# Nine pairs of the down projection get high and low part of the weights by DMA, and ten pairs use seven products

## The chip, the cores and the metric

The kernel runs on one core of a Trainium2 chip. The metric is device time in microseconds (us), from one launch of the whole program. Several engines run side by side on the core: TensorE (PE, its weight loads are shown as PEld), VectorE (DVE), ScalarE (ACT), GpSimd (POOL) and SyncE (SP). Each takes its own instructions in the order in which the program lists them. SP, ACT and POOL can also issue DMA transfers; these run on 16 DMA engines that all issuers share.

## The reference

One decoder layer on 256 tokens of width 2048: differential attention beside a pooling mixer, cross-attention into 256 memory tokens, then a SwiGLU feed-forward part with 5632 inner features, and a last RMSNorm. What matters here is the feed-forward part:

```
def _swiglu(h, w_gate, w_up, w_down):
    return (jax.nn.silu(h @ w_gate) * (h @ w_up)) @ w_down
...
hf = _rmsnorm(x, norm_ffn[l])
x = x + _swiglu(hf, w_gate[l], w_up[l], w_down[l])
return _rmsnorm(x, norm_final)
```

The change concerns the product with `w_down` (5632 by 2048), the last large product of the layer.

## The kernel before

All matrix products run in a rounded 32-bit format (float32r). To keep accuracy each operand is split into a high part (the value rounded to that format) and a low part (the value minus the high part), and a product is made of three matmuls: high by high, high by low, low by high. `split` does that: ACT writes the high part (line 129), DVE subtracts it from the source (line 130). `mm3` issues the three matmuls (lines 217 to 219), each 128 by 128 against 512 columns in the down projection.

Down projection: the 2048 output columns are done in two blocks `b` of 1024, and the 5632 inner features are 44 tiles of 128, taken as 22 pairs `p`. For each pair and block one transfer of 1 MB brings four weight pieces of 512 columns each (`raw`, line 706, issued on SP; `raw` has three buffers). `prep` yields split pieces, and the loop at line 783 issues the products:

- An ordinary pair needs 8 block products (2 token halves, 2 column halves, 2 feature tiles), so 24 matmuls. Its weights are two splits of two pieces each (line 719 and 720).
- A pair in `FAST` uses a Strassen-like scheme with 7 block products, so 21 matmuls. Its weights need three sums and differences more on DVE (`less`, line 716), and four splits. The activations of such a pair were combined beforehand in `pair_of`.

In the kernel before, `FAST` is 2, 4, ... 18 (nine pairs); the 13 others are ordinary. So seven-product pairs and ordinary pairs alternate for most of a block. Split weights lie in `whi` and `wlo` with three buffers each. A tile framework adds the waits: an instruction that writes a buffer waits until the readers of its earlier contents are done. The order on each engine is fixed when the program is built.

Of the kernel before, what the change touches and what calls it, by code (L numbers as in the profile page):

```python
# [24 lines left out]
F32 = mybir.dt.float32  # L25
F32R = mybir.dt.float32r
AF = mybir.ActivationFunctionType
ALU = mybir.AluOpType
# [3 lines left out]
P = 128  # L32
# [11 lines left out]
FP = FT // 2  # L44
NB = D // 512

FAST = tuple(range(2, 20, 2))


C_MIX, C_XAT, C_MEM, C_FFN, C_FIN, C_SUB, C_PSC, C_LAM = 0, 16, 32, 48, 64, 80, 82, 90  # L50
# [5 lines left out]
def layer_kernel(ctx: ExitStack, tc: tile.TileContext, a: dict, out: bass.AP):  # L56
    nc = tc.nc
# [23 lines left out]
    def name(n):  # L81
        uid[0] += 1
        return f"{n}{uid[0]}"
# [14 lines left out]
    def t1():  # L98
        return tmp.tile([P, S], F32, tag="t1", bufs=6, name=name("t1_"))
# [235 lines left out]
    v = [values(ps_v0, rc_x), values(ps_v1, rc_x)]  # L335
# [6 lines left out]
    for g, w in enumerate(WINDOWS):  # L342
# [5 lines left out]
        for kt in range(2):  # L348
            b, dgn = t1(), t1()
# [346 lines left out]
    dec = ctx.enter_context(tc.tile_pool(name="dec", bufs=3, side="right", reuse_waits="tile"))  # L696
# [5 lines left out]

    def prep(b, p):

        raw = wts.tile([P, 4, 512], F32, tag="raw", name=name("raw"))
        nc.sync.dma_start(out=raw.rearrange("p s n -> p (s n)"), in_=a["w_dn"][b, p])
        b11, b22, b21, b12 = (raw[:, i] for i in range(4))

        def parts(src, n=2):
            hi = wts.tile([P, 1024], F32R, tag="whi", name=name("whi")).rearrange("p (s n) -> p s n", s=2)  # L710
            lo = wts.tile([P, 1024], F32R, tag="wlo", name=name("wlo")).rearrange("p (s n) -> p s n", s=2)
            split(hi[:, :n], lo[:, :n], src)
            return [(hi[:, i], lo[:, i]) for i in range(n)]

        def less(o, x, y):
            nc.vector.tensor_tensor(out=o, in0=x, in1=y, op=ALU.subtract)

        if p not in FAST:
            yield parts(raw[:, 0:2])
            yield parts(raw[:, 2:4])  # L720
            return
        yield parts(raw[:, 0:2])
        s = dec.tile([P, 2, 512], F32, tag="sum", bufs=2, name=name("sum"))
        less(s, b12[:, None].to_broadcast([P, 2, 512]), raw[:, 0:2])
        yield parts(s)
        less(b12, b22, s[:, 0])
        yield parts(raw[:, 2:4])
        less(b22, b21, b12)
        yield parts(raw[:, 1:2], 1)

    def finished(b, t, h):

# [41 lines left out]
    for b in range(2):  # L774
        M = {}
        C = [acc() for _ in range(4)]

        def into(ps, w, n, p, last=False):
            mm3(ps, sides[p][n], w, id(ps) not in M, last or (p in FAST[-1:] and any(ps is q for q in shared)))
            M[id(ps)] = True  # L780

        shared = [misc() for _ in range(4)] if FAST else []
        for p in range(FP):
            parts = prep(b, p)
            if p in FAST:
                b11, b22 = next(parts)
                into(shared[0], b11, A11, p)
                into(C[1], b22, S4, p)
                s1, s3 = next(parts)
                tick()  # L790
                into(shared[1], s1, S1, p)
                into(shared[3], s3, S3, p)
                b21, s2 = next(parts)
                into(C[0], b21, A12, p)
                into(shared[2], s2, S2, p)
                s4, = next(parts)
                tick()
                into(C[2], s4, A22, p)
            else:
                b11, b22 = next(parts)  # L800
                tick()
                into(C[0], b11, A11, p)
                into(C[2], b11, A21, p)
                into(C[1], b22, A12, p)
                into(C[3], b22, A22, p)
                b21, b12 = next(parts)
                tick()
                last = p == FP - 1
                into(C[0], b21, A12, p, last)
                into(C[1], b12, A11, p, last)  # L810
                into(C[2], b21, A22, p, last)
                into(C[3], b12, A21, p, last)
            if p == 8 or (not FAST and p == 0):
                between.append(load_rows(b))
            if b == 1 and p == 9:
                between.append(load_gains())
            if p in FAST[-1:]:
                between.append(sums(b, [shared[0], None, shared[1], shared[2], shared[3]]))
        finish()
        for i, ps in enumerate(C):  # L820
            y = ys[b][i // 2][:, (i % 2) * 512:(i % 2 + 1) * 512]
            nc.vector.tensor_tensor(out=y, in0=ps, in1=y, op=ALU.add)
            if b:
                finished(b, i // 2, i % 2)
        if b == 0:
            def late():
                for _ in range(26):
                    yield

                nc.scalar.activation(out=ss[:, :, 0], in_=ss[:, :, 0], func=AF.Sqrt)  # L830
                for i in range(4):
                    finished(0, i // 2, i % 2)
                    yield
            nc.vector.memset(ss, 1.0)
            between.append(late())
# [90 lines left out]
```

## Time and profile before

| | |
|---|---|
| median of 3 runs | 1423.15 us (1422.8 to 1424.44) |
| the profiled execution's own time | 1424.28 us |
| its span, first to last instruction | 1422.6 us |
| PE busy | 1404.4 us, 99% |
| DVE busy | 967.5 us, 68% |
| ACT busy | 742.3 us, 52% |
| POOL busy | 23.6 us, 2% |
| mean DMA rate | 193 GB/s |

Busy time of PE overlaps from one matmul to the next, so it is not a sum of costs: what a matmul costs when many follow each other is the distance between their starts. The granted TensorE clock was 1.00 of full speed (2.4 GHz) through the stage that is changed.

### The profile page before, as it was taken

Reading aid. Unit: us, or ns where it says so; the run is one execution under the profiler, and the core shown is the slowest. Engines: PE = TensorE matmul, PEld = TensorE weight load, DVE = VectorE, ACT = ScalarE, POOL = GpSimd, SP = SyncE. Lnnn points to the kernel's source line nnn. Section 1 sums busy time; section 2 is a strip of 40 time slices with the busy share of each in tenths; the row PEclk is TensorE's granted clock in tenths of the full one; section 3 lists DMA queues with packets and bytes.
Section 4 is the critical chain, followed back from the end, with each engine's and each line's share of the span. In section 5 each row is a group of like instructions: output and inputs, shape, how many; then the busy total and the mean of one; then the engine's idle time right before and its main releaser. Section 6 shows DMA issues by size and latency. Waiting matters only on the chain.

```text
span 1422.6 us, 19276 instructions
## 1 busy us (share of the span) xinstructions
PE 1404.4 (99%) x7610; PEld 1208.7 (85%) x7610; DVE 967.5 (68%) x1361; ACT 742.3 (52%) x1083; POOL 23.6 (2%) x55
## 2 busy tenths in 40 slices
PE   8999999999999999999999999999999999999996
PEld 7788888888888888888888888888888888888784
DVE  6666868765555655566666666666666668887985
ACT  6555756555445444455545444554445544555554
POOL 1200000000000000000000000000000000000000
PEclk9999999999999999999999999999999999999998
DMA  9555437565554445465655555555555556566662
GB/s 342 185 178 172 170 125 256 203 237 191 194 178 151 175 152 177 134 234 200 200 186 199 180 199 184 189 196 180 201 181 193 192 183 219 192 209 236 211 212 107
DMA packets 43147, 273.93 MB, mean 193 GB/s; under 512 B 4912, under 2 KB 5936, under 8 KB 12848
## 3 DMA queue, kind: packets, MB, share of 16 engines
q1 hardware_dynamic: 40608, 266.36, 54.1%
q10 hardware_dynamic: 2448, 6.34, 1.2%
q8 instruction: 59, 0.97, 0.3%
q14 instruction: 32, 0.26, 0.1%
HBM read 268.48 MB, written 4.19 MB: 192 GB/s over the span
## 4 chain that ended last, share of the span: by engine, by line
PE 93%; DVE 2%; DMA 2%; ACT 1%; POOL 1%; issue 0%; SPq 0%; DVEq 0%
PE acc L163 44%; PE acc L164 22%; PE acc L218 4%; PE acc L219 4%; PE acc L210 4%; PE acc L211 4%; PE acc L209 3%; PE acc L217 3%; PE ms L218 2%; PE ms L219 2%; PE ms L217 2%; DVE wlo L130 1%; DMA raw<-in_w_dn 1%; DMA raw<-in_w_vu 1%; ACT whi L129 0%
## 5 line engine op out<-in xcount | busy, mean ns | idle before, releaser
L130 DVE TENSOR_TENSOR wlo<-raw,whi 128x1024 fp32r<-128x1024 f32 (+1 forms) x510 | 606.5, 1196 | 360.7 <-ACT whi L129 357.6
L129 ACT CAST whi<-raw 128x1024 fp32r<-128x1024 f32 (+1 forms) x510 | 523.2, 1029 | 527.0 <-PE acc L163 250.6
L163 PE MATMUL acc<-hid,whi 128*128 128x512 f32 x1920 | 670.7, 393 | 0.0
L164 PE MATMUL acc<-hid,wlo 128*128 128x256 f32 x1920 | 538.1, 280 | 0.0
L163 PEld LDWEIGHTS acc<-hid,whi 128*128 128x128 f32 x1920 | 359.6, 187 | 80.8
L164 PEld LDWEIGHTS acc<-hid,wlo 128*128 128x128 f32 x1920 | 362.9, 189 | 0.0
L163 PE MATMUL acc<-act,whi 128*128 128x512 f32 x768 | 271.9, 398 | 0.0
L164 PE MATMUL acc<-act,wlo 128*128 128x256 f32 x768 | 215.5, 281 | 0.0
L163 PEld LDWEIGHTS acc<-act,whi 128*128 128x128 f32 x768 | 144.2, 188 | 34.0
L164 PEld LDWEIGHTS acc<-act,wlo 128*128 128x128 f32 x768 | 145.1, 189 | 0.2
L218 PE MATMUL acc<-wlo,aC 128*128 128x512 f32 x208 | 83.1, 399 | 0.4
L219 PE MATMUL acc<-whi,aC 128*128 128x512 f32 x208 | 81.2, 390 | 0.0
L217 PE MATMUL acc<-whi,aC 128*128 128x512 f32 x208 | 75.2, 390 | 0.0
L210 PE MATMUL acc<-wlo,hid 128*128 128x512 f32 x128 | 50.5, 395 | 1.6 <-DVE wlo L130 1.5
L209 PE MATMUL acc<-whi,hid 128*128 128x512 f32 x128 | 50.2, 394 | 1.6 <-ACT whi L129 1.5
L218 PEld LDWEIGHTS acc<-wlo,aC 128*128 128x128 f32 x208 | 39.0, 188 | 13.2 <-DVE wlo L130 5.7
L209 PE MATMUL acc<-whi,act 128*128 128x512 f32 x128 | 50.0, 390 | 0.0
L210 PE MATMUL acc<-wlo,act 128*128 128x512 f32 x128 | 49.9, 390 | 0.0
L211 PE MATMUL acc<-whi,hid 128*128 128x512 f32 x128 | 49.8, 389 | 0.0
L211 PE MATMUL acc<-whi,act 128*128 128x512 f32 x128 | 49.8, 389 | 0.0
L129 ACT CAST act<-t 128x256 fp32r<-128x256 f32 x48 | 19.5, 406 | 54.9 <-DVE t L225 54.9
L217 PEld LDWEIGHTS acc<-whi,aC 128*128 128x128 f32 x208 | 39.0, 188 | 8.8 <-DVE t1f L653 0.2
(189 smaller groups left out, 1266.8 us busy)
## 6 DMA issues: line engine op xcount, KB each, us to landing
raw<-in_w_gu SPq DMA_DIRECT2D x88, 1024.0 KB, 4.8
raw<-in_w_dn SPq DMA_DIRECT2D x44, 1024.0 KB, 4.8
raw<-in_w_qk SPq DMA_DIRECT2D x16, 1024.0 KB, 4.8
raw<-in_w_qx SPq DMA_DIRECT2D x16, 1024.0 KB, 4.8
raw<-in_w_kx SPq DMA_DIRECT2D x16, 1024.0 KB, 4.9
raw<-in_w_vx SPq DMA_DIRECT2D x16, 1024.0 KB, 4.8
raw<-in_w_vu SPq DMA_DIRECT2D x12, 1024.0 KB, 4.9
raw<-in_w_o SPq DMA_DIRECT2D x12, 1024.0 KB, 5.0
```

The source lines that it names most:

```text
L129: nc.scalar.copy(out=hi, in_=src)
L130: nc.vector.tensor_tensor(out=lo, in0=src, in1=hi.bitcast(F32), op=ALU.subtract)
L163: nc.tensor.matmul(ps, whi[:, w], x, start=(k == 0), stop=False)
L164: nc.tensor.matmul(ps[:, :S], wlo[:, w], x[:, 0], start=False, stop=(k == nk - 1))
L209: nc.tensor.matmul(ps[t], xh, whi[:, w], start=(k == 0), stop=False)
L210: nc.tensor.matmul(ps[t], xh, wlo[:, w], start=False, stop=False)
L211: nc.tensor.matmul(ps[t], xl, whi[:, w], start=False, stop=(k == KT - 1))
L217: nc.tensor.matmul(ps, l[0], r[0], start=start, stop=False)
L218: nc.tensor.matmul(ps, l[0], r[1], start=False, stop=False)
L219: nc.tensor.matmul(ps, l[1], r[0], start=False, stop=stop)
```

## The change

`FAST` becomes the odd pairs 1, 3, ... 19: ten instead of nine. A new list `ADDED` holds the even pairs 2, 4, ... 18, nine pairs that stay ordinary but get their parts in another way. Pairs 0, 20 and 21 are ordinary as before.

For a pair in `ADDED` there is no `raw` transfer, no cast on ACT and no subtraction on DVE. Instead `by_dma`, called one pair earlier in program order, does this for each of the two halves of 1024 columns (512 KB): a DMA issued on POOL loads the weights from memory into `phi` and rounds them on the way (float32 to float32r); ACT writes the negated high part into `plo`; a second DMA on POOL loads the same weights again and adds them to `plo`, which leaves weights minus high part. `phi` and `plo` have three buffers each, so one and a half pairs. To make room, the buffer `sum` of the seven-product pairs goes from two to one.

```
-FAST = tuple(range(2, 20, 2))
+FAST = tuple(range(1, 21, 2))
+
+ADDED = tuple(range(2, 19, 2))
...
     def prep(b, p):
 
+        if p in ADDED:
+            for hi, lo in added.pop(0):
+                yield [tuple(v[:, i * 512:(i + 1) * 512] for v in (hi, lo)) for i in range(2)]
+            return
         raw = wts.tile([P, 4, 512], F32, tag="raw", name=name("raw"))
...
-        s = dec.tile([P, 2, 512], F32, tag="sum", bufs=2, name=name("sum"))
+        s = dec.tile([P, 2, 512], F32, tag="sum", bufs=1, name=name("sum"))
...
+    added = []
+
+    def by_dma(b, p):
+
+        w = []
+        src = a["w_dn"][b, p]
+        for h in range(2):
+            hi = dec.tile([P, 1024], F32R, tag="phi", bufs=3, name=name("phi"))
+            lo = dec.tile([P, 1024], F32R, tag="plo", bufs=3, name=name("plo"))
+            nc.gpsimd.dma_start(out=hi, in_=src[:, h * 1024:(h + 1) * 1024])
+            w.append((hi, lo))
+        for h, (hi, lo) in enumerate(w):
+            nc.scalar.activation(out=lo, in_=hi.bitcast(F32), func=AF.Copy, scale=-1.0)
+            nc.gpsimd.dma_start(out=lo, in_=src[:, h * 1024:(h + 1) * 1024], accum_op=ALU.add)
+        added.append(w)
...
         for p in range(FP):
+            if p + 1 in ADDED:
+                by_dma(b, p + 1)
             parts = prep(b, p)
```

How the order on the engines changes, at three places. In these rows the number behind a name tells one tile from the next; L131 and L132 are the two lines of `split` in the changed kernel, L746 the casting DMA, L749 the negation, L750 the adding DMA.

POOL, which has nothing to do in the down projection before, in the middle of block 0 of the changed kernel. `phi_11002` and `phi_11005` are the halves of pair 8, `phi_11079` and `phi_11082` those of pair 10.

```order
L750 DMA plo_11003<-in_w_dn 128x1024 [waits DMASW0_49,Activation_49]
L746 DMA phi_11005<-in_w_dn 128x1024 [waits DMASW7_49,PE_49]
L746 DMA phi_11079<-in_w_dn 128x1024 [waits DMASW2_49,PE_49]
L750 DMA plo_11006<-in_w_dn 128x1024 [waits DMASW1_49,Activation_49]
L750 DMA plo_11080<-in_w_dn 128x1024 [waits DMASW4_49,Activation_49]
L746 DMA phi_11082<-in_w_dn 128x1024 [waits DMASW3_49,PE_49]
```

Each casting DMA waits for PE (the buffer's last reader, three halves earlier: for the second half of pair 8 that is the first half of pair 6), and each adding DMA waits for ACT. They stand in one queue, two and two by turns.

ACT at the same place. Before, around pairs 5 (raw_10924, ordinary) and 6 (raw_10958, seven products):

```order
L129 CAST whi_10926<-raw_10924 128x1024 [waits DMAHW4_49,DVE_49,PE_49]
L129 CAST whi_10942<-raw_10924 128x1024 [waits DVE_49,PE_49]
L129 CAST whi_10960<-raw_10958 128x1024 [waits DMAHW5_49,DVE_49,PE_49]
L129 CAST whi_10972<-sum_10970 128x1024 [waits DVE_49,PE_49]
L129 CAST whi_10983<-raw_10958 128x1024 [waits DVE_49,PE_49]
L129 CAST whi_10994<-raw_10958 128x512 [waits DVE_49,PE_49,Activation_49]
```

In the changed kernel, around pair 7 (raw_11012, seven products), with the negations of pair 8 between its casts:

```order
L131 CAST whi_11014<-raw_11012 128x1024 [waits DMAHW2_49,DVE_49,PE_49]
L749 ACTIVATE plo_11003<-phi_11002 128x1024 [waits DMASW3_49,DMASW0_49]
L131 CAST whi_11026<-sum_11024 128x1024 [waits DVE_49,PE_49]
L131 CAST whi_11037<-raw_11012 128x1024 [waits DVE_49,PE_49]
L749 ACTIVATE plo_11006<-phi_11005 128x1024 [waits DMASW6_49,DMASW1_49,PE_49]
L131 CAST whi_11048<-raw_11012 128x512 [waits DVE_49,PE_49,Activation_49]
L131 CAST whi_11091<-raw_11089 128x1024 [waits DMAHW4_49,DVE_49,PE_49]
```

The two casts of the ordinary pair are gone. In their place stand two negations, each of which waits for a casting DMA (a DMASW semaphore); the second of them stands ahead of the last cast of pair 7.

ACT at the start of block 0 of the changed kernel: raw_10781 is pair 1, raw_10858 pair 3, phi_10771 and phi_10774 are pair 2, phi_10848 is the first half of pair 4.

```order
L131 CAST whi_10806<-raw_10781 128x1024 [waits DVE_49,PE_49,Activation_49]
L749 ACTIVATE plo_10772<-phi_10771 128x1024 [waits DMASW0_49]
L131 CAST whi_10817<-raw_10781 128x512 [waits DVE_49,PE_49,Activation_49]
L131 CAST whi_10860<-raw_10858 128x1024 [waits DMAHW7_49,DVE_49,PE_49]
L749 ACTIVATE plo_10775<-phi_10774 128x1024 [waits DMASW1_49]
L749 ACTIVATE plo_10849<-phi_10848 128x1024 [waits DMASW2_49]
```

The negation of pair 2's second half stands behind the first cast of pair 3, which needs a `whi` buffer that PE frees only in the middle of pair 1.

## Rows read from the trace of the kernel before

**Rows 1.** The page: span, and busy time by engine.

```profile
span 1422.6 us, 19276 instructions
...
PE 1404.4 (99%) x7610; PEld 1208.7 (85%) x7610; DVE 967.5 (68%) x1361; ACT 742.3 (52%) x1083; POOL 23.6 (2%) x55
```

**Rows 2.** Windows over the down projection: busy time by engine, clock, DMA.

```profile
core 0: us, PE busy (x) PEld busy (x) DVE busy (x) ACT busy (x) POOL busy (x), PEclk, DMA share, GB/s
1177.40:1291.00 113.60, 113.53 (x495) 91.73 (x494) 94.54 (x100) 61.03 (x65) 0.00 (x0) 1.00 0.61 211
1291.00:1408.70 117.70, 117.39 (x510) 94.52 (x509) 99.22 (x107) 62.66 (x73) 0.00 (x0) 1.00 0.54 190
...
1235.03:1245.36 10.33, 10.33 (x47) 8.37 (x45) 8.80 (x10) 5.80 (x7) 0.00 (x0) 1.00 0.58 201
```

**Rows 3.** Matmuls on the tile aC, min/median/max ns, first and last start.

```profile
L217 PE MATMUL acc<-whi,aC x208: 387/389/462, 1177.5 to 1408.3; 128*128 128x512 f32 x104
...
L219 PE MATMUL acc<-whi,aC x208: 387/389/402, 1178.0 to 1408.7; 128*128 128x512 f32 x104
```

**Rows 4.** Matmuls on the tile aS of the seven-product pairs, likewise.

```profile
L217 PE MATMUL ms<-whi,aS x72: 389/389/390, 1188.5 to 1391.1; 128*128 128x512 f32 x72
...
L217 PE MATMUL acc<-whi,aS x54: 388/389/392, 1189.2 to 1391.7; 128*128 128x512 f32 x54
```

**Rows 5.** Timeline of PE: start, duration, matmul; one ordinary and one seven-product pair.

```profile
1235.03 0.84 PE L217 MATMUL acc<-whi,aC 128*128 128x512 f32 x3
1235.71 0.50 PE L218 MATMUL acc<-wlo,aC 128*128 128x512 f32 x1
...
1237.20 0.39 PE L217 MATMUL acc<-whi,aC 128*128 128x512 f32 x1
...
1240.60 0.39 PE L217 MATMUL ms<-whi,aS 128*128 128x512 f32 x1
...
1245.13 0.39 PE L219 MATMUL acc<-whi,aS 128*128 128x512 f32 x1
```

**Rows 6.** Waits in 1170 to 1423 us: total, times, longest.

```profile
PEld acc L218 <- DVE wlo L130: 6.4, 20, 0.6
```

**Rows 7.** Groups by form, 1177 to 1423 us: busy, mean ns, idle before.

```profile
L130 DVE TENSOR_TENSOR wlo<-raw,whi 128x1024 fp32r<-128x1024 f32 x87 | 104.5, 1220 | 28.6 <-ACT whi L129 28.4
L129 ACT CAST whi<-raw 128x1024 fp32r<-128x1024 f32 x86 | 88.8, 1054 | 65.2 <-PE acc L219 44.8 <-PE ms L219 14.6 <-DVE sum L716 3.0
...
L716 DVE TENSOR_TENSOR sum<-raw 128x1024 f32<-128x1024 f32 x18 | 21.9, 1219 | 1.8 <-DMA raw<-in_w_dn 1.2 <-PE acc L164 0.5
...
L130 DVE TENSOR_TENSOR wlo<-raw,whi 128x512 fp32r<-128x512 f32 x18 | 12.3, 684 | 0.0
...
L129 ACT CAST whi<-raw 128x512 fp32r<-128x512 f32 x18 | 11.2, 622 | 5.5 <-PE acc L219 5.5
...
L843 ACT ACTIVATE y<-y,r 128x1024 f32<-128x1024 f32 x2 | 2.2, 1142 | 0.0
```

**Rows 8.** DMA queues and issues: issuer, count, size, median us to landing.

```profile
q1 hardware_dynamic: 40608, 266.36, 54.1%
q10 hardware_dynamic: 2448, 6.34, 1.2%
...
raw<-in_w_dn SPq DMA_DIRECT2D x44, 1024.0 KB, 4.8
...
y<-x_dram ACTq DMA_DIRECT2D x4, 512.0 KB, 6.2
...
g<-in_gain ACTq DMA_DIRECT2D x2, 512.0 KB, 3.7
```

**Rows 9.** The window with the highest DMA rate, near the program's start.

```profile
20.00:30.00 10.00, 9.43 (x40) 7.52 (x41) 7.44 (x9) 6.44 (x9) 0.00 (x0) 1.00 1.01 419
```

More of the change, by code (lines that the diff above doesn't have):

```diff
@@ L812, in layer_kernel @@
                 into(C[3], b12, A21, p, last)
-            if p == 8 or (not FAST and p == 0):
+            if p == 8:
                 between.append(load_rows(b))
```

## The prediction, made before the changed kernel ran

> **What bounds the kernel now.** I read the page first: PE is busy for 99% of the span and POOL for 2% [rows 1], so a gain has to come out of PE's own time, and POOL is a free issuer. Then I cut out the stage that changes. The matmuls of the down projection start at 1177.5 us and the last starts at 1408.7 us [rows 3]. There are three lines with 208 matmuls on `aC` each [rows 3] and 72 + 54 on `aS` each [rows 4], so 3 x 334 = 1002 matmuls, as 2 x (13 x 24 + 9 x 21) says. Next the timeline: from 1237.20 to 1245.13 stand 36 matmul starts, so 35 steps of 7.93 / 35 = 0.2266 us [rows 5]. That is what a matmul costs when nothing is late. 1001 steps would be 226.8 us; the stage took 231.2 us. PE therefore loses only 4.4 us here, and the waits name the one cause: weight loads that need `wlo`, 20 times, 6.4 us in total [rows 6] (more than is lost, since a weight load that waits a little still lies under the running matmul). They occur where an ordinary pair begins: in the timeline three L217 are taken early and the first L218 follows late [rows 5]. DVE is the late one: in a calm period of one ordinary and one seven-product pair it is busy 8.80 of 10.33 us, ACT 5.80 [rows 2]. The DMA engines are at 0.54 to 0.61 of their time and 190 to 211 GB/s in the stage [rows 2].
>
> **The change, part by part.**
>
> *Matmuls.* One pair more has seven products: 3 matmuls fewer in each block, 6 x 0.2266 = 1.4 us off PE. This part is sure.
>
> *DVE and ACT work.* Per period DVE loses two subtractions of 1.22 us and keeps three of 1.22 us, one of 0.68 us, one `sum` of 1.22 us and two half-wide differences that I take at 0.68 us each like the half-wide subtraction [rows 7]: 6.9 us of about 10.2. ACT loses two casts of 1.05 us and gains two negations; the nearest row is the 128x1024 ACTIVATE with 1.14 us [rows 7], so ACT stays near 6 us. With DVE relieved and no `wlo` needed in the ordinary pairs, most of the 4.4 us of waits should go: I take -4.0 us, with bounds 0 and -4.4 us. A single `sum` buffer costs nothing as long as DVE has 3 us to spare in a period; that cover is the reason for 0.
>
> *DMA traffic.* Now the other side. Per period the engines move 1 MB of `raw`, 1 MB for `phi`, 1 MB again for `plo`, and to add they must also fetch what lies in `plo`, another 1 MB inside the core: 3 MB from memory or 4 MB of reads, against 2 MB before. The highest rate in this trace is 419 GB/s [rows 9], 2.50 us per MB. So 7.5 us or 10.0 us of engine time in a period of 45 matmuls, 45 x 0.2266 = 10.2 us: from a share near 0.6 to between 0.73 and 0.98. The second figure leaves nothing to hide a delay in.
>
> The Trainium skill, page "Collectives: The Full Stack", section "The bandwidth ceiling: the fold count and why AG ≠ RS ≠ AR", says that an add in the DMA path is not slow for its arithmetic but because it reads two sources, and so delivers about half. By that rule the 10.0 us would hold and not the 7.5; no row of this trace shows an adding DMA.
>
> *The chain through the buffers.* Let T be the moment when PE is done with the first half of an `ADDED` pair, say pair 6. Only then may POOL issue the cast for the second half of pair 8 (it is that buffer's next owner). Then follow: casting DMA, negation on ACT, adding DMA; and PE wants the result after 12 matmuls (second half of pair 6), 21 (pair 7) and 12 (first half of pair 8): 45 x 0.2266 = 10.20 us after T. The negation takes 1.14 us [rows 7], so the two transfers of 512 KB have 9.06 us between them. What one takes: nothing in this trace is issued on POOL, casts or adds (both queues are hardware ones of SP and ACT [rows 8]), so I bound it. From below, the 512 KB load in a quiet stretch took 3.7 us; from above, the 512 KB load of `y` beside weight transfers took 6.2 us [rows 8]. Twice the low value gives 7.4 us, below 9.06, no wait. Twice the high value gives 12.4 us, 3.3 us too late in each period. The engines will be busier than they were around the `y` loads, so the adding DMA, with its second read, I put at 6.2 us; the casting one midway, 5.0 us. Sum 11.2 us, 2.14 us late. This recurs for pairs 4 to 18 of each block, 16 times (the first halves in a block are loaded during the pairs without `ADDED`): 16 x 2.14 = 34.2 us; bounds 0 and 16 x 3.3 = 53 us with plain-copy prices, and more if casting or adding is slower than copying.
>
> Where that wait shows: ACT takes its instructions in order, and the negation of pair 8's second half stands ahead of the last cast of pair 7. That cast, 0.62 us, and its subtraction, 0.68 us [rows 7], must be done when PE has taken 12 + 18 matmuls after T, at 6.80 us. With the negation, the casting DMA may take 6.80 - 1.14 - 0.62 - 0.68 = 4.36 us; at 5.0 us PE waits 0.64 us there for `wlo`, and the remaining 1.5 us at the second half of pair 8 for `plo`. It is not paid twice, since a wait at the first place gives the adding DMA the same time back.
>
> *The start.* In block 0 the memory of `phi` is that of the up projection, so pair 2 can't be loaded ahead. Its second negation stands behind the first cast of pair 3, which waits for the second part of pair 1: 1177.4 + 36 x 0.2266 = 1185.6 us, plus 1.05 + 1.14 = 1187.8 us, plus 3.7 to 6.2 us for the adding DMA = 1191.5 to 1194.0 us. PE, without a wait, is there after 24 + 21 + 12 matmuls, at 1190.3 us. So 1.2 to 3.7 us; I take 2.5 us.
>
> *Up projection.* One pair more is combined with four small DVE operations; DVE is busy for about two thirds of the span [rows 1], and PE hides it. 0.
>
> **Sum.** -1.4 - 4.0 + 34.2 + 2.5 = +31.3 us. On the profiled execution's own 1424.28 us that is 1455.6 us; this execution lies 1.1 us over the median of the runs, so against 1423.15 us I forecast 1454 us. The last stretch after the final matmul stays as it is.
>
> **The rivals.**
>
> *All hidden.* If the two transfers together stay below 9.06 us, only -5.4 us and the start remain: 1418 to 1421 us. For it: the quiet 3.7 us, and 1.7 us of slack at that price. Against it: it needs nearly quiet engines at a load of 0.73 or more. The point that decides is sharp: at 9.4 us together the loss is 16 x 0.34 = 5.4 us, and the gain is gone.
>
> The Trainium skill, page "DMA: Bandwidth & Descriptors", section "Anatomy of one DMA — SWDGE (gpsimd) path", gives 2.0 us plus bytes over 436 GB/s for a transfer issued on GpSimd; as an estimate 3.2 us for 512 KB, two of them 6.4 us, and all would be hidden. No row here shows that path.
>
> *Casting or adding runs below copy speed.* Then the DMA engines themselves set the period. With the add at half its speed a period is 2.5 + 2.5 + 10.0 = 15.0 us, 4.8 us more than 10.2; with cast and add both at half speed 2.5 + 5.0 + 10.0 = 17.5 us, 7.3 us more. Over 18 periods +86 to +131 us, 1510 to 1555 us. For it: neither operation is in this trace, so nothing says they run at copy speed; against it nothing either.
>
> *DVE relief brings nothing.* The waits on `wlo` move from the ordinary to the seven-product pairs, whose casts now share ACT with negations. That costs the 4.0 us: 1458 us, inside my case's own range.
>
> **How the numbers follow.** The case I forecast has 2 x 5.0 to 2 x 6.2 us for the two transfers, so +15 to +53 us on a base of -2.9 us: 1435 to 1473 us, with a chance of 0.47. All hidden: 0.12. Between 9.2 and 9.6 us together, where loss and gain cancel: 0.13. Below copy speed: 0.28. A measurement of this kernel tells a change of about 0.2% (2.8 us) from none. So faster 0.12, same 0.13, slower 0.75. For eight in ten the range goes from 1421 us, which leaves out most of the hidden case, to 1555 us, which leaves out slowdowns beyond half speed.
>
> **What the profile would show.** Right: 996 matmuls still at 0.2266 us when they run; in the waits of the stage a new line, PE weight loads waiting for `plo` by DMA, 16 times around 1.5 us, and some for `wlo` behind ACT; ACT waiting for `phi`; a DMA share above 0.75; DVE near 7 us per period. The time from issue to landing of `phi` and `plo` decides it: together 11.2 us by my account. Wrong: if they land within 9 us of each other's sum, PE runs through and the kernel is faster by some 4 us; if `plo` takes 10 us and more, the stage is bound by the DMA engines and my size is far too small.

## The result, and the profile after

The changed kernel took 1502.62 us (median of 4 runs, 1499.08 to 1507.03), the kernel before 1422.97 us beside it (median of 4 runs). The ratio is 1.0561, with a 95% interval from 1.0531 to 1.0592: slower by 79.6 us. The forecast was 1454 us, 31 us slower; 1502.62 us lies inside its range of 1421 to 1555 us, but the loss is two and a half times the forecast one. It lies outside the 1435 to 1473 us of the case that was forecast; only the rival *below copy speed* (1510 to 1555 us) stretched the range so far.

The page of the changed kernel's profile answers to [rows 1, 8]: span, busy time by engine, the queues, and the issues with their median time to landing.

```profile
span 1501.5 us, 19352 instructions
...
PE 1427.7 (95%) x7604; PEld 1218.8 (81%) x7604; DVE 939.8 (63%) x1338; ACT 740.6 (49%) x1086; POOL 75.4 (5%) x127
...
q0 software_dynamic: 10368, 37.75, 10.9%
...
raw<-in_w_dn SPq DMA_DIRECT2D x26, 1024.0 KB, 8.6
phi<-in_w_dn POOLq DMA_DIRECT2D x36, 512.0 KB, 6.3
plo<-in_w_dn POOLq DMA_DIRECT2D x36, 512.0 KB, 8.1
```

There are six matmuls fewer, as said, and a new queue. The casting DMA (`phi`) lands after 6.3 us where I took 5.0, the adding one (`plo`) after 8.1 us where I took 6.2, and the ordinary `raw` load, 4.8 us before [rows 8], now needs 8.6 us.

The waits of the changed kernel in its last 337 us (total, times, longest) answer to [rows 6].

```profile
ACT plo L749 <- DMA phi<-in_w_dn: 80.1, 18, 8.8
PEld acc L220 <- DMA plo<-in_w_dn: 48.0, 18, 5.3
...
PEld acc L219 <- ACT whi L131: 13.3, 8, 2.6
...
PE acc L219 <- ACT whi L131: 9.9, 8, 2.2
...
PEld acc L220 <- DVE wlo L132: 5.9, 11, 0.7
...
PE acc L220 <- DVE wlo L132: 2.3, 10, 0.3
```

PE's weight loads wait for the adding DMA 18 times: 16 as forecast (pairs 4 to 18 of both blocks), two more at the start (both halves of pair 2 in block 0). ACT's negations wait 80.1 us for the casting DMA. The 13.3 us, and nine of the eleven waits in the 5.9 us, are at the other forecast place, the last cast of a seven-product pair behind the second negation on ACT. The weight loads wait partly under a running matmul; the matmuls themselves lose 9.9 and 2.3 us there.

The windows show the start (pair 2 of block 0), eight periods of block 0, and one stretch inside them.

```profile
1182.00:1202.08 20.08, 12.53 (x45) 8.87 (x44) 13.56 (x15) 8.51 (x9) 5.06 (x7) 0.92 0.89 242
1202.08:1320.78 118.70, 94.89 (x356) 72.80 (x357) 52.26 (x54) 43.97 (x48) 23.01 (x32) 0.90 0.79 205
1260.00:1270.00 10.00, 7.80 (x22) 6.20 (x23) 1.41 (x3) 1.68 (x2) 1.46 (x2) 0.66 0.72 202
```

Eight periods take 118.70 us, 14.84 us each where 45 undelayed matmuls take 10.20. DVE is busy for 52.26 / 8 = 6.5 us of each, so it is relieved as forecast, and the DMA engines are at 0.79 of their time although they deliver only 205 GB/s, no more than before [rows 2].

One chain, word for word, from the timeline of all engines (start, duration, engine, work, and the idle time before it with what ended it).

```profile
1258.68 0.55 POOL L746 DMA_DIRECT2D phi<-in_w_dn  x1 [1.45 <-PE acc L221]
...
1262.20 0.29 PEld L220 LDWEIGHTS acc<-plo,aC 128*128 128x128 f32 x1 [4.03 <-DMA plo<-in_w_dn]
...
1266.62 1.06 ACT L749 ACTIVATE plo<-phi 128x1024 fp32r<-128x1024 f32 x1 [8.70 <-DMA phi<-in_w_dn]
...
1268.10 0.92 POOL L750 DMA_DIRECT2D plo<-in_w_dn  x1
...
1276.42 0.19 PEld L220 LDWEIGHTS acc<-plo,aC 128*128 128x128 f32 x1 [1.43 <-DMA plo<-in_w_dn]
```

PE frees the buffer of pair 10's first half, and POOL issues the cast of pair 12's second half at 1258.68. It lands 7.94 us later, the negation takes 1.06, POOL is free for the adding DMA 0.42 us after that, and its data are there at 1276.42, 8.32 us after its issue: 17.74 us in all. Measured so, from the casting DMA's issue to PE's first weight load of `plo`, the 16 chains last 13.16 to 19.84 us, 16.74 us in the mean: 7.61 us for the casting DMA, 1.06 for the negation, 0.48 until POOL issues the add, 7.58 for the adding DMA. My forecast had 11.2 + 1.14 = 12.34 us. POOL's own queue, in which the add stands behind the next casting DMA, thus adds little.

**How such a chain turns into time.** The line at 1262.20 shows what my sum missed. It is PE waiting for pair 10's second half, and pair 12's chain was already running for 3.5 us, because it starts at the end of the *first* half of pair 10, ahead of that wait. A wait thus gives the next chain a head start. Call W the moment at which PE gets a second half, c the chain, and e what else holds PE in a period. Then the chain that ends at one W starts 10.20 us + e after the W two places before it, so two periods last 10.20 + e + c, and one lasts (10.20 + e + c) / 2, as long as PE waits each time. To c belong 0.25 us more, the delay from PE's last matmul to POOL's issue. This delay and e together can be read from the 14 chains that have a W two places before in their block: the casting DMA's issue less that W less 10.20 us is 2.31 us in the mean. With c = 16.74 us this gives (10.20 + 2.31 + 16.74) / 2 = 14.6 us; measured are 14.84 us in block 0 and, from pair 4 to 18 of block 1 (W at 1368.89 and 1469.31), 14.35 us. The relation only writes the program's order as a sum: it says how a long chain becomes time, not why the chain is long. Most of e is what PE loses at `whi` and `wlo` (9.9 + 2.3 us) and by its clock (16 us, below), 1.8 us in each of 16 periods.

**The clock.** PE's timeline just behind the wait of 1262.20:

```profile
1258.21 0.39 PE L219 MATMUL acc<-phi,aC 128*128 128x512 f32 x1
1262.20 0.80 PE L220 MATMUL acc<-plo,aC 128*128 128x512 f32 x1 [3.60 <-DMA plo<-in_w_dn]
1262.80 0.63 PE L221 MATMUL acc<-phi,aC 128*128 128x512 f32 x1
1263.22 0.63 PE L219 MATMUL acc<-phi,aC 128*128 128x512 f32 x1
```

After 3.60 us without work matmuls start 0.42 us apart in place of 0.23, and the granted clock of 1260 to 1270 us is 0.66, a mean of full speed and the lower level of 1.2 GHz. 88 weight loads of the stage run wholly or partly at the lower level, which adds some 16 us over the usual distance of their matmuls. My sum had no such term. By the relation above it counts only half: while PE is slow, the next chain runs on.

**The account.** The undelayed stage would be 995 x 0.2266 = 225.5 us; from 1177.6 to the last start at 1487.3 it took 309.7, so 84.2 us are lost. PE reaches the second half of pair 2 at 1202.08, and undelayed it would after 58 matmuls, at 1190.7: the start costs 11.4 us. Block 0's eight periods cost 118.70 - 81.6 = 37.1 us. The rest, 35.7 us, falls between 1320.78 and 1469.31: again 8 late chains, with some 3 us at the change of blocks. Less the 4.4 us that the stage lost before and the 1.4 us of six matmuls, that is +78.4 us; the two profiled executions are 1503.25 - 1424.28 = 79.0 us apart.

### The profile page after: what moved, and what is told of

It is laid out like the page before. It is cut to its first block, busy times and chain, and to the rows that moved or that the text cites. A ratio compares the mean times of both kernels' runs of the same rounds, so it can differ in the third digit from the quotient of the medians.

```text
span 1501.5 us, 19352 instructions
## 1 busy us (share of the span) xinstructions
PE 1427.7 (95%) x7604; PEld 1218.8 (81%) x7604; DVE 939.8 (63%) x1338; ACT 740.6 (49%) x1086; POOL 75.4 (5%) x127
## 4 chain that ended last, share of the span: by engine, by line
PE 75%; issue 14%; POOL 4%; DMA 3%; DVE 2%; ACT 1%; SPq 0%; POOLq 0%; ACTq 0%; DVEq 0%
PE acc L165 40%; PE acc L166 21%; PE acc L212 3%; PE acc L213 3%; PE acc L211 3%; POOL plo L750 2%; POOL phi L746 1%; DMA act<-in_memT 1%; PE ms L221 1%; PE ms L220 1%; PE ms L219 1%; DMA plo<-in_w_dn 1%; DVE wlo L132 1%; DMA phi<-in_w_dn 1%; ACT whi L131 1%
## 5 line engine op out<-in xcount | busy, mean ns | idle before, releaser
L132 DVE TENSOR_TENSOR wlo<-raw,whi 128x1024 fp32r<-128x1024 f32 (+1 forms) x476 | 567.1, 1193 | 454.7 <-ACT whi L131 451.5
L131 ACT CAST whi<-raw 128x1024 fp32r<-128x1024 f32 (+1 forms) x476 | 486.4, 1024 | 489.5 <-PE acc L165 255.5
L220 PE MATMUL acc<-plo,aC 128*128 128x512 f32 x144 | 63.9, 443 | 40.4 <-DMA plo<-in_w_dn 40.4
L749 ACT ACTIVATE plo<-phi 128x1024 fp32r<-128x1024 f32 x36 | 38.0, 1057 | 129.6 <-DMA phi<-in_w_dn 80.1
L746 POOL DMA_DIRECT2D phi<-in_w_dn x36 | 20.0, 558 | 1117.8 <-DVE aC L132 989.0
L220 PEld LDWEIGHTS acc<-plo,aC 128*128 128x128 f32 x144 | 29.8, 207 | 54.2 <-DMA plo<-in_w_dn 48.0
L219 PE MATMUL acc<-phi,aC 128*128 128x512 f32 x144 | 60.2, 420 | 2.8 <-DMA phi<-in_w_dn 2.8
L221 PE MATMUL acc<-phi,aC 128*128 128x512 f32 x144 | 61.8, 429 | 0.0
```

The costliest lines, as they stand in the source:

```text
L131: nc.scalar.copy(out=hi, in_=src)
L132: nc.vector.tensor_tensor(out=lo, in0=src, in1=hi.bitcast(F32), op=ALU.subtract)
L219: nc.tensor.matmul(ps, l[0], r[0], start=start, stop=False)
L220: nc.tensor.matmul(ps, l[0], r[1], start=False, stop=False)
L221: nc.tensor.matmul(ps, l[1], r[0], start=False, stop=stop)
L746: nc.gpsimd.dma_start(out=hi, in_=src[:, h * 1024:(h + 1) * 1024])
```

## The experiments

My theory after this was the forecast's chain through three buffers, with longer transfers. Its rivals were the order on ACT, the throughput of the DMA engines, and DVE or matmul effects of the ten seven-product pairs. The first question was whether the other parts of the change do anything, and what a few added pairs cost. Where a ratio with its interval stands, the time is the median of 4 executions (12 for `e_ten`); the other times are of one execution each. Those of the changed kernel lie 8 us apart, so smaller differences are not read from single ones.

**Ten seven-product pairs alone** (`e_ten`):

```
-ADDED = tuple(range(2, 19, 2))
+ADDED = ()
```

> Ten pairs with seven products, but no pair gets its parts by DMA (the other twelve are ordinary, as before), one sum buffer. Theory (the loss is all in the DMA parts): 6 matmuls fewer, -1.4 us, and about the 4 us of waits for wlo of the kernel before: 1421 to 1423 us. Rival (ten seven-product pairs or the single sum buffer make DVE late): more waits for wlo, 5 us and more, 1427 us or above.

1424.22 us, ratio 1.0000 (0.9991 to 1.0008). The six matmuls saved are taken back by waits, of which this line of the wait view tells:

```profile
PEld acc L220 <- DVE wlo L132: 7.1, 22, 0.7
```

So the whole loss comes from the nine pairs by DMA.

**Four added pairs a block** (`e_four`), far enough apart that each has two periods:

```
-ADDED = tuple(range(2, 19, 2))
+ADDED = (4, 8, 12, 16)
```

> The changed kernel with only pairs 4, 8, 12 and 16 by DMA, so a buffer has 90 matmuls, 20.4 us, from release to use instead of 45 and 10.2 us; the others are ordinary. Theory 1 (only the chain through the three buffers costs): 6.3 + 1.1 + 8.1 us fit into 20.4 us, no wait for plo, 1418 to 1421 us, faster than before. Theory 2 (the negation in ACT's fixed order also holds PE): the negation of the second half of the next DMA pair still stands ahead of the last cast of the seven-product pair that follows an added pair, and may be ready at most 4.4 us after the release; with 5 to 6 us to landing PE waits 1 to 2 us for whi and wlo, 7 times, while plo never waits: 1425 to 1433 us. Rival (casting and adding cost the same wherever they stand): 8/18 of the 80 us, some 1455 us.

1443.33 us, ratio 1.0136 (1.0121 to 1.0151). PE never waits for `plo` any more, but 21 times for `wlo`, 23.6 us. The timeline shows why:

```profile
1244.19 1.22 DVE L722 TENSOR_TENSOR sum<-raw 128x1024 f32<-128x1024 f32 x1 [2.60 <-DMA raw<-in_w_dn]
...
1246.06 2.95 DVE L132 TENSOR_TENSOR wlo<-raw,whi 128x1024 fp32r<-128x1024 f32 x3
1247.33 0.19 PEld L220 LDWEIGHTS acc<-wlo,aS 128*128 128x128 f32 x1 [3.13 <-DVE wlo L132]
```

DVE stands at the first sum of the next seven-product pair, whose `raw` load is late, and the last two subtractions of the pair that PE is at stand behind it in DVE's program; PE waits for the first of them (1246.06 to 1247.28). It is DVE's order, not ACT's, that passes the lateness on. My second theory named the wrong engine, and its 1425 to 1433 us were too low; none of the three ranges was met.

**A fourth `raw` buffer for that kernel** (`e_raw4`). Here and below memory is made by a smaller unused pad (`PAD`, two tiles at the ends of the memory), which moves the addresses of everything between:

```
-PAD = (144, 248)
+PAD = (8, 104)
...
+        loads[0] += 1
+        if loads[0] % 4 == 0:
+            raw = dec.tile([P, 4, 512], F32, tag="rawd", bufs=1, name=name("rawd"))
+        else:
+            raw = wts.tile([P, 4, 512], F32, tag="raw", name=name("raw"))
```

> Pairs 4, 8, 12 and 16 by DMA as in e_four, and a fourth buffer for raw (every fourth load goes into it), so that the sum of the next seven-product pair, which stands on DVE ahead of the last subtraction of the one before, finds its weights landed. Theory (in e_four PE lost its 25 us because DVE stood before a late raw load with that subtraction behind it): the waits for wlo of 2.4 to 3.3 us go, 1418 to 1425 us. Rival (the adds slow the raw loads so that one buffer more doesn't help): 1435 us and more.

1444.2 us, ratio 1.0133 (1.0116 to 1.0150): no gain, although the waits on `wlo` fell from 23.6 to 9.7 us. What ate it was ahead of the stage: the first matmul of the down projection came at 1183.4 us in place of 1177. Whether the buffer or the addresses did that was told apart by **the same kernel with other pads** (`e_raw4q`):

```
-PAD = (8, 104)
+PAD = (8, 64)
```

> Four added pairs a block and a fourth buffer for raw, as before, but with the two pad tiles of 8 and 64 in place of 8 and 104 columns, so that only addresses change. Theory 1, addresses slowed the matmuls there: their median distance falls from 0.394 to 0.389 us durations, the first matmul of the down projection starts near 1177 to 1179 us in place of 1183, and the time is 5 to 9 us lower, 1435 to 1439 us, and so 5 us or more below the kernel with four added pairs and three raw buffers (1443 us), because the late raw loads no longer hold DVE. Theory 2, the fourth buffer and not the address slowed them: 1444 us as before, and the first matmul at 1183 us.

1437.82 us, ratio 1.0109 (1.0092 to 1.0126), 6.4 us less. The same line of the matmul view (ns min/median/max, first and last start) in the kernel with 104 columns:

```profile
L219 PE MATMUL acc<-whi,aC x128: 388/394/503, 1183.4 to 1427.9; 128*128 128x512 f32 x128
```

and in the one with 64:

```profile
L219 PE MATMUL acc<-whi,aC x128: 387/390/502, 1178.7 to 1419.3; 128*128 128x512 f32 x128
```

So addresses alone slowed the matmuls. The other traces agree: all three kernels with pads of 8 and 104 have this median at 394 ns and start the stage at 1183.2 to 1184.8 us, the four with 8 and 64 have 389 or 390 ns and start at 1178.0 to 1178.7. The time shows it less surely, since the kernel before also ran 2.5 us faster beside `e_raw4q` than beside `e_raw4`, and the two intervals overlap. Against `e_four` it is 5.5 us less; how much of that is the late `raw` loads is not separated, since the addresses differ as well. The waits left are 12.6 us for `wlo`. A variant with the negations held back as well (`e_raw4p`; its edit is that of `e_pin4` below, two pairs back in place of three, with the pads of `e_raw4q`)

> As e_raw4, with each negation held back until the last cast of the ordinary pair two pairs earlier, so that ACT doesn't stand before phi either. If ACT's order still costs something in e_raw4, this is faster by 5 to 15 us and reaches 1416 to 1421 us; if not, the two are within 2 us of each other.

took 1444.88 us, ratio 1.0124 (1.0095 to 1.0154), so holding back gained nothing over `e_raw4q`: held back that far, the adding DMA is late itself, and PE waits for `plo` 15 times, 20.0 us.

**What the transfers cost by themselves** (`micro`), each after the one before it, then casts and adds beside a stream of 1 MB loads on SP:

```
last[0] = one("plc", F32, 1024, lambda t: nc.gpsimd.dma_start(out=t, in_=src(1024)))
last[0] = h = one("cst", F32R, 1024, lambda t: nc.gpsimd.dma_start(out=t, in_=src(1024)))
last[0] = one("add", F32R, 1024, lambda t: nc.gpsimd.dma_start(out=t, in_=src(1024), accum_op=ALU.add), neg=h)
```

> Leaves out the whole layer: it only times transfers one after the other, each issued when the one before has landed, with all engines quiet: 512 KB on SP (sph), 1 MB on SP (spf), 512 KB plain on POOL (plc), casting on POOL (cst), adding on POOL (add); then casting (cstr) and adding (addr) beside a stream of 1 MB loads on SP. Theory 1 (casting and adding run near copy speed, and in the kernel the crowd makes them slow): quiet sph 3.4 to 3.8 us, cst 4 to 4.5, add 5 to 5.5; beside the stream 6 and 8. Theory 2 (the operations are slow by themselves): quiet cst 6 and add 8, like in the kernel, with the stream more.

The issues on its page (`sph` and `spf` are plain loads on SP, `plc` a plain one on POOL, `cstr` and `addr` a cast and an add beside streams of 1 MB loads, `rawa` the stream of the casts):

```profile
rawa<-in_w_dn SPq DMA_DIRECT2D x10, 1024.0 KB, 6.6
spf<-in_w_dn SPq DMA_DIRECT2D x6, 1024.0 KB, 4.7
sph<-in_w_dn SPq DMA_DIRECT2D x6, 512.0 KB, 3.7
plc<-in_w_dn POOLq DMA_DIRECT2D x6, 512.0 KB, 4.1
cst<-in_w_dn POOLq DMA_DIRECT2D x6, 512.0 KB, 4.0
add<-in_w_dn POOLq DMA_DIRECT2D x6, 512.0 KB, 5.5
cstr<-in_w_dn POOLq DMA_DIRECT2D x5, 512.0 KB, 6.4
addr<-in_w_dn POOLq DMA_DIRECT2D x5, 512.0 KB, 9.9
```

Its windows, one transfer in each (`spf`, `plc`, `cst`, `add`); the last two columns are the share of the DMA engines and GB/s:

```profile
80.36:85.74 5.38, 0.00 (x0) 0.20 (x1) 0.00 (x0) 1.00 0.59 195
85.74:90.33 4.59, 0.00 (x0) 0.20 (x1) 0.55 (x2) 1.00 0.39 114
90.33:95.86 5.53, 0.00 (x0) 1.06 (x1) 0.53 (x2) 1.00 0.32 95
95.86:101.74 5.88, 0.00 (x0) 0.20 (x1) 0.88 (x1) 1.00 0.50 89
```

Share times length is the time of all engines that a transfer takes: 1.79 us for the copy, 1.77 for the cast, 2.94 for the add, 3.17 for 1 MB; the other rounds give 1.67 to 1.79, 1.77 to 1.89, 2.94 to 3.20 and 2.83 to 3.17. So casting costs hardly more than copying; adding costs 1.4 times the time to landing and about 1.7 times the engines. Beside the stream a cast takes 6.4 us and an add 9.9 us.

**The second DMA without its add** (`e_noadd`):

```
-nc.gpsimd.dma_start(out=lo, in_=src[:, h * 1024:(h + 1) * 1024], accum_op=ALU.add)
+nc.gpsimd.dma_start(out=lo, in_=src[:, h * 1024:(h + 1) * 1024])
```

> The changed kernel with the second DMA of each half as a plain casting one that overwrites the negated high part instead of adding to it (the low part is then wrong; order, waits and bytes from memory stay). Theory (the adding itself, with its second read, is what makes plo slow): plo lands in about the 6.3 us of phi instead of 8.1 us, and the waits for plo, 47 us, fall by 1.8 us and more each: 1460 to 1475 us. Rival (POOL's way of issuing, or the crowd on the DMA engines, makes both slow): plo still takes some 8 us, 1490 to 1505 us.

1458.0 us, 44.6 us less than the changed kernel with the same number of transfers from memory, and 2 us below the theory's range. Its issues, beside 8.6, 6.3 and 8.1 us in the changed kernel:

```profile
raw<-in_w_dn SPq DMA_DIRECT2D x26, 1024.0 KB, 6.5
phi<-in_w_dn POOLq DMA_DIRECT2D x36, 512.0 KB, 5.3
plo<-in_w_dn POOLq DMA_DIRECT2D x36, 512.0 KB, 5.7
```

The adding is thus worth more than half of the loss, through all three. Whether its second read or the addition itself is the price, this run does not tell apart.

**Fewer `raw` loads** (`e_thin`): only the first seven-product pair of a block loads its weights, the others use them again.

```
+        if p in FAST[1:]:
+            raw = kept[0]
+        else:
+            raw = wts.tile([P, 4, 512], F32, tag="raw", name=name("raw"))
+            nc.sync.dma_start(out=raw.rearrange("p s n -> p (s n)"), in_=a["w_dn"][b, p])
```

> The changed kernel in which only the first seven-product pair of a block loads its 1 MB of raw weights and the nine others compute on with that tile (their weights are then wrong; orders on ACT and POOL, DVE's work and all transfers for phi and plo stay). It takes away the other traffic beside the chain. Theory (the raw loads crowd the chain's transfers): phi falls from 6.3 us to 4.5 to 5, plo from 8.1 to 6 to 6.5, chain 1.1 + 10.5 to 11.5 against 10.2, so 1.5 to 2.5 us late in a period instead of over 4: 1440 to 1465 us. Rival 1 (phi and plo crowd each other): landing times hardly fall, 1485 us and more. Rival 2 (quiet transfers would fit): 1420 us.

1461.6 us, 41 us less, with `phi` at 5.2 and `plo` at 5.7 us. The chain is still the limit, as its timeline of all engines shows:

```profile
1236.45 0.55 POOL L752 DMA_DIRECT2D phi<-in_w_dn  x1 [1.01 <-PE acc L221]
1237.41 0.19 PEld L220 LDWEIGHTS acc<-plo,aC 128*128 128x128 f32 x1 [1.46 <-DMA plo<-in_w_dn]
...
1249.02 0.19 PEld L220 LDWEIGHTS acc<-plo,aC 128*128 128x128 f32 x1 [1.52 <-DMA plo<-in_w_dn]
```

The chain lasts 1249.02 - 1236.45 = 12.57 us, almost what I forecast for the changed kernel, and the period 1249.02 - 1237.41 = 11.61 us. The relation gives (10.20 + 12.57 + 0.25) / 2 = 11.5 us, with an e near nothing; my forecast's rule, 10.20 us plus all that the chain is late, would give 12.8. Over the eight periods of block 0 the chains last 13.35 us in the mean and a period 12.30; the relation gives 11.9 us plus half of e. So it holds at a second length of chain.

**A fourth buffer** for `phi` and `plo` (`e_b4`) frees the buffer of a second half 33 matmuls, 7.5 us, earlier:

```
-PAD = (144, 248)
+PAD = (8, 104)
...
-            hi = dec.tile([P, 1024], F32R, tag="phi", bufs=3, name=name("phi"))
-            lo = dec.tile([P, 1024], F32R, tag="plo", bufs=3, name=name("plo"))
+            hi = dec.tile([P, 1024], F32R, tag="phi", bufs=4, name=name("phi"))
+            lo = dec.tile([P, 1024], F32R, tag="plo", bufs=4, name=name("plo"))
```

> The changed kernel with four buffers each for phi and plo (the memory comes from the two pad tiles), so a half has 78 matmuls, 17.7 us, from the buffer's release to its use instead of 10.2. Theory 1 (three buffers alone cost the time): no wait for plo, 1418 to 1425 us. Theory 2 (behind it stands ACT's order: the negations now stand even earlier, ahead of casts of the seven-product pair, and wait for phi): waits for plo gone, but waits for whi and wlo of 1 to 2.5 us in most periods, 1440 to 1465 us. Rival (the DMA engines can't move it in 10.2 us a period): 1480 us and more, with a DMA share near 1.

1497.67 us, of which some 6 us are those pads (its down projection starts at 1183.2 us). That is above theory 2's range and inside the rival's, but the share that the rival asked for is not there: the DMA engines are at 0.84 from 1210 to 1330 us. Its waits:

```profile
PEld acc L219 <- ACT whi L131: 34.4, 12, 7.1
PEld acc L220 <- DVE wlo L132: 8.5, 14, 2.0
PEld acc L220 <- DMA plo<-in_w_dn: 7.8, 2, 5.7
```

The wait for `plo` is gone but for the start, and the wait behind ACT has taken its place: the negation still waits for the casting DMA (6.8 us here, up to 12.1), and the casts of the seven-product pair stand behind it. The chain is one limit with a second close behind.

**The negation on POOL**, so that ACT has nothing to wait for, with four buffers (`e_pneg4`, pads of 8 and 104) and with three (`e_pneg3`):

```
-            nc.scalar.activation(out=lo, in_=hi.bitcast(F32), func=AF.Copy, scale=-1.0)
+            nc.gpsimd.tensor_scalar(out=lo, in0=hi.bitcast(F32), scalar1=-1.0, scalar2=None, op0=ALU.mult)
```

> Four buffers as in the run before, and the negation on POOL instead of ACT, so that no cast on ACT stands behind a wait for a transfer. Theory (buffers and ACT's order together are the loss): PE hardly waits, 1418 to 1428 us, if POOL's negation takes below 2 us. Rival (throughput of the DMA engines): 1470 us and more.

> Three buffers, negation on POOL. Theory (the chain through three buffers sets the period, ACT's order only shifts where PE waits): waits for whi behind ACT (13 us) go, waits for plo grow by as much or by more, since POOL's negation also holds its queue: 1495 to 1520 us. Rival (ACT's order was the main loss): 1440 us or less.

1531.01 and 1532.94 us. PE's waits for `whi` behind ACT fall to 2.7 and 1.6 us, but POOL takes 3.02 and 2.98 us for the same negation and holds up its own next issues with it; PE waits for `plo` for 70.8 and 72.2 us. Neither number was foreseen: I had no row for POOL at this work. The first of the two also says nothing on throughput, since its theory asked for a negation below 2 us.

**Four buffers, and each negation held back on ACT** until the casts of the pair three places earlier are done (`e_pin4`, pads of 8 and 64): the scale -1 of the negation is read from a column that ACT writes there.

```
+                pins[p] = dec.tile([P, 1], F32, tag="pin", bufs=4, name=name("pin"))
+                nc.scalar.activation(out=pins[p], in_=hi[:, 0, :1].bitcast(F32), func=AF.Copy, scale=0.0, bias=-1.0)
...
-            nc.scalar.activation(out=lo, in_=hi.bitcast(F32), func=AF.Copy, scale=-1.0)
+            nc.scalar.activation(out=lo, in_=hi.bitcast(F32), func=AF.Copy, scale=pins[p - 3] if p - 3 in pins else -1.0)
```

> Four buffers each for phi and plo, and each negation held back until the last cast of the seven-product pair three pairs earlier (its factor -1 is a column that ACT writes after that cast, one small ACT instruction a pair), so that no cast that PE needs soon stands behind a wait for phi. Both obstacles of the order are then gone. Theory 1 (only buffers and order): 1418 to 1425 us. Theory 2 (the DMA engines are the next limit): quiet, the transfers of a period took 3.1 us for raw, 2 x 1.8 for the casts and 2 x 3.3 for the adds as share times duration, 13.3 us against a period of 10.2; overlap makes up some of it, so 11 to 13 us a period, share near 1, waits for plo or raw of 1 to 3 us a period: 1435 to 1470 us.

1468.99 us, the fastest kernel with all nine pairs done in full. Three windows of one period each:

```profile
1230.12:1241.87 11.75, 10.92 (x45) 8.31 (x46) 6.71 (x7) 5.83 (x7) 2.90 (x4) 1.00 0.99 272
1241.87:1253.48 11.61, 10.94 (x45) 8.29 (x45) 6.71 (x7) 5.84 (x7) 2.85 (x4) 1.00 1.03 269
1253.48:1265.90 12.42, 11.20 (x45) 8.23 (x45) 6.71 (x7) 5.75 (x7) 2.86 (x4) 1.00 0.96 256
```

In them the DMA engines are full, at 256 to 272 GB/s, and a period needs 11.6 to 12.0 us of them (share times length). In the changed kernel it is 0.79 x 14.84 = 11.7 us, in the kernel before 0.58 x 10.33 = 6.0 [rows 2]. Two things went otherwise than expected. PE hardly waits for `plo` or `raw`, but for `wlo` (21.8 us) and `whi` (13.7 us): the negations still wait for late casting DMAs, 84.9 us on ACT, and casts stand behind them, so full engines reach PE through ACT's order. And three of the 16 periods last 15.9 to 19.2 us at a share of only 0.80 to 0.85, the last one of block 0 and the second and third measured in block 1; throughput is not what limits these.

**The same without the add** (`e_pin4n`, edit as in `e_noadd`):

> As the kernel with four buffers and negations held back, but the second DMA overwrites its target and does not add, so that the low part of the nine pairs is wrong (it holds the weights); this leaves out the second read of the add. Theory 1, behind buffers and order the DMA engines' throughput is the limit: their quiet engine time per period falls from 13.3 to 10.3 us (transfers measured alone: 3.1 + 2 x 1.8 + 2 x 1.8), the share falls below 0.95, the period returns to 10.2 to 10.5 us, and the time is 1428 to 1440 us (what is left is the start of the blocks). Theory 2, the order and the late negations set the period of 12 us there: the period stays near 11.5 us or more and the time is 1452 us or more.

1449.8 us, between the two ranges. Two windows of 72 us, seven periods in block 0 and six in block 1:

```profile
1204.00:1276.00 72.00, 72.00 (x313) 58.35 (x312) 45.56 (x47) 39.10 (x46) 14.79 (x28) 1.00 0.91 293
1336.00:1408.00 72.00, 66.04 (x270) 49.52 (x270) 42.00 (x47) 34.20 (x42) 11.95 (x23) 1.00 0.87 269
```

In block 0 PE runs through without a gap, 10.37 us a period, with the DMA engines at 0.91, so 9.4 us per period. In these periods full engines were all that was left behind buffers and order. In block 1 a period still lasts about 12 us at a share of 0.87: PE waits two or three times in each for `wlo`, up to 1.5 us. Longer than that it waits once at the end of block 0 (5.5 us for `whi`). Why block 1 differs I did not settle, so of the roughly 45 us by which `e_pin4` is slower than the kernel before, about 19 are shown to be the add's price. What is left without the add is the start (6.7 us), the end of block 0 (8.0) and block 1 (14), counted against undelayed matmuls or, at the end of block 0, the other periods.

No kernel was faster than the one before; `e_ten` is level with it.

## Why the prediction was right in direction and wrong in size

The path was right: the chain through three buffers, with PE waiting for `plo` 16 times. What failed is the size of its term, +34.2 us, which measured some 70 us: the two transfers were priced too low, and the rule that turned lateness into time was not the right one.

- **Matmuls, -1.4 us: right.** 996 matmuls. Alone with the new waits it is worth 0 (`e_ten`).
- **DVE relief, -4.0 us:** DVE fell to 6.5 us a period, against 6.9 forecast. The gain can't be seen by itself, since PE's lost 4.4 us gave way to larger waits.
- **The chain, +34.2 us: right mechanism, the term mis-sized.** It is some 70 us (37.1 in block 0, 35.7 in block 1 with about 3 us at the change of blocks); by the relation 54 of them are the chain itself and 16 are e. Two steps of it failed, in opposite directions. The first is the choice of 5.0 and 6.2 us for the two transfers: they took 6.3 and 8.1 us in the median, and with the negation and the time on POOL the chain was 16.74 us, not 12.34. I had priced them by plain loads at the old load of the engines, while the added traffic itself slowed them: quiet they take 4.0 and 5.5 us, and without the `raw` loads 5.2 and 5.7 (`e_thin`). The second is "16 x 2.14": a wait gives the next chain a head start, so a chain of 12.34 us would itself have cost only half of 2.14 us a period, some 17 us; the period of `e_thin` with 12.57 us shows that. Against this the sum had nothing for e. In `e_noadd` the 16 chains last 12.36 us in the mean, the forecast's length, and its periods cost 29 us in all, 19 by the chain with its 0.25 us of delay and 10 by e: at that length the 34.2 us would have come near by two errors that cancel, and that would have been luck.
- **The order on ACT:** its waits are there as forecast, larger (13.3 us for `whi` where I had 0.64 us each time). "Not paid twice" was half right: they are part of e, and e counts half.
- **The start, +2.5 us:** 11.4 us. POOL's first cast waited for DVE's last operation of the up projection until 1182.47 us, and then three casts, three adds and `raw` ran at once, at a share of 0.89; the add for pair 2's second half took 9.6 us from its issue, where I allowed 3.7 to 6.2.
- **The clock:** no term in my sum, and no reason given for that; about 16 us of slower matmuls, counting half.
- **The rivals.** *All hidden* and *cancel* fell. *Below copy speed* had its reason half right: casting runs at copy speed, adding does not; 1502.62 us lies near its range without its mechanism, since the engines were at 0.79 and did not set the period. The 11.7 us of engine time per period exceed 10.20 us, so by these figures no order or number of buffers could have hidden all of the change; but this limit sits behind the chain and ACT's order, and `e_pin4` is where it shows. My two figures for it were 7.5 and 10.0 us.

The Trainium skill, page "Collectives: The Full Stack", section "The bandwidth ceiling: the fold count and why AG ≠ RS ≠ AR", says of a reduce-scatter that its add in the DMA path needs two source reads and so delivers about half. The runs agree in kind: 2.94 against 1.77 us of engine time, 0.6 of the cast's rate. By that rule I should have let the 10.0 us, and not the 7.5, raise the transfers' prices.

The Trainium skill, page "DMA: Bandwidth & Descriptors", section "Anatomy of one DMA — SWDGE (gpsimd) path", gave an estimate of 3.2 us for 512 KB; a quiet copy on POOL took 4.1 us, so the measurement decides against that figure. The all-hidden case falls even with quiet engines: a cast and an add took 4.0 + 5.5 = 9.5 us, above the 9.06 us that it allowed.

## What to carry to other kernels

Work moved from a busy engine to the DMA engines is priced by what all transfers of a period take of the engines together: if that sum passes the period, buffers and order cannot hide it all (here the best of them took back 34 of the 80 us). Count an adding DMA as more than a copy (here 1.7 times), and price every transfer at the load that exists after the change, the untouched ones too. For a chain through a ring of buffers write down which earlier moment starts it; here each wait gave the next chain a head start, so the loss per period was half of what the chain was late, plus half of what else held PE.

## What the runs showed of the hardware that was not expected

- TensorE's granted clock fell after a wait of 3.60 us, and matmuls then started 0.42 us apart in place of 0.23.
- Moving addresses by a smaller pad alone (64 in place of 104 columns) changed the median matmul from 394 to 390 ns and brought the start of the down projection forward by 4.7 us. Which address does it was not tried.
- POOL took 2.98 us to negate 128x1024 values (`e_pneg3`), ACT 1.06 us.
- An instruction that issues an adding DMA occupies POOL for 0.88 us, a casting or plain one for 0.55.
